# Two heads stacked in 64 columns instead of block-diagonal in 128, in the chunk chain of a decoder layer

## The chip, the core and the metric

The kernel runs on one core of a Trainium2 chip. The core has a matrix engine (PE, with its weight loads shown apart as PEld), three engines for elementwise work (DVE, ACT and POOL), and queues that start transfers between device memory and on-chip memory (SBUF). Matrix products land in PSUM, which PE writes and DVE and ACT read. Every engine works off its own instructions in a fixed order. A wait of one instruction therefore holds up all that stand behind it on that engine. The metric is the device time of one execution in microseconds (us).

## The reference

One decoder layer over 512 positions with 2048 features: a mixing sub-layer and a feed-forward sub-layer, each with a conditioned norm ahead and a gated residual add behind. Half of the mixing features run through a gated linear recurrence (RG-LRU), the other half through 16 heads of 64 features with a matrix state. This second recurrence is what the change touches:

```python
def step(state, inp):
    r_t, d_t, k_t, v_t, kk_t, a_t = inp
    sa = jnp.einsum('bhvk,bhk->bhv', state, -kk_t)
    state = (state * d_t[:, :, None, :]
             + sa[..., None] * (kk_t * a_t)[:, :, None, :]
             + v_t[..., None] * k_t[:, :, None, :])
    y_t = jnp.einsum('bhvk,bhk->bhv', state, r_t)
    return state, y_t
```

## The kernel before

The large products (input projection, output projection, feed-forward) are written as three matmuls each on a rounded and a remainder part of both operands (`mm3`, lines 124 to 126). Their weights are streamed in. ACT rounds a weight tile (L105) and DVE takes the remainder (L106).

The matrix-state recurrence runs over 8 pairs of heads. One head of a pair has partitions 0 to 63, the other 64 to 127. The 512 positions are cut into 8 chunks of 64, four to a half. For each half of a pair `rwkv_half` builds the operands. `bd_a`, `bd_bt`, `bd_v` and `bd_xt` are block-diagonal tiles of 128 columns a chunk, one 64 by 64 block for each head and zeros elsewhere. `inverse` finds the inverse of a triangular 32 by 32 block by 31 steps of two short DVE instructions each (L764 and L766), in which each step needs the one before. The transposed input of the steps is the tile `rw_at` (L757), their result is transposed to `rw_xn` (L768), and PE needs that for L783.

`rwkv_chain` then goes over the chunks. Each has four links: `w` (L694, L696, copied out by ACT at L698), `u` (L701, copied out at L703), the new state (L708, L709, combined on DVE at L720 with the old state scaled by ACT at L719), and three matmuls into the output `yps` (L710, L712, L713). All eight matmuls take 128 by 128 weights. `w`, `u` and the state are 128 columns wide, and the output matmuls move 64 columns.

The order is written by `weave`. It goes round five generators (the chain, the two halves, the pair's set-up, and the modulation columns) and a filler, which is the large products. Each generator yields how long PE is thought to work and how long its result is thought to take. Until that time is over, filler is put in, three matmuls at a time. The recording layer then moves instructions of each engine by its own estimates, so the final order is not the written one. PSUM tile `ch` has two buffers.

## Time and profile before

| | |
|---|---|
| median of 3 runs | 2511.21 us (2509.33 to 2516.2) |
| profiled execution | 2503.34 us, span 2501.5 us |
| PE busy, whole span | 2403.7 us (96%) |
| DVE busy, whole span | 1380.6 us (55%) |
| stage of the recurrence | 250 to 915 us |
| PE, DVE, ACT, POOL busy in that stage | 638.14, 566.14, 326.33, 71.67 of 665 us |

A matmul on plain 32-bit operands appears as two records with two weight loads, so "x2" in the timeline is one matmul of the program. The end of a matmul is modelled, and starts of successive matmuls tell more about their price than durations. "PE busy" therefore covers small gaps between starts.

### The profile page before, as it was taken

To read this page: it belongs to the slowest core of one execution; us is meant where nothing else is said; L and a number is where in the kernel's file an instruction comes from. 1 tells how busy PE (TensorE), PEld (TensorE's weight loads), DVE (VectorE), ACT (ScalarE), POOL (GpSimd) and SP (SyncE) were. 2 spreads that over 40 slices of the span, in tenths; PEclk is the share of its full clock that TensorE was granted. 3 is DMA by queue.
4 is the path that set the end of the run, shared out by engine and by line. 5 is a ranking of instruction groups with operands and counts; after the bars stand their busy time and mean duration, and the time that the engine had idled before them with its cause. 6 is when DMAs were issued, how large, how long until landed. Compare 5 with 4: busy or idle time off the path is not lost.

```text
span 2501.5 us, 30983 instructions
## 1 busy us (share of the span) xinstructions
PE 2403.7 (96%) x11560; PEld 1951.2 (78%) x11560; DVE 1380.6 (55%) x3111; ACT 843.9 (34%) x1340; POOL 82.5 (3%) x131
## 2 busy tenths in 40 slices
PE   6999999999999999999999999999999999999997
PEld 3677777877777877788788888888888888888885
DVE  7879898999979838855423322233322233222244
ACT  4357364465365333422222222222222222222221
POOL 0000111111101100000000000000000000000000
PEclk9999999999999999999999999999999999999998
DMA  8864444444442438366423332323333233332233
GB/s 313 307 220 129 146 126 152 130 150 150 132 129 88 136 118 286 105 213 203 149 86 96 107 98 97 99 85 95 109 98 97 91 93 107 98 99 96 86 95 114
DMA packets 138938, 333.22 MB, mean 133 GB/s; under 512 B 15458, under 2 KB 28898, under 8 KB 134690
## 3 DMA queue, kind: packets, MB, share of 16 engines
q1 hardware_dynamic: 138788, 331.25, 41.0%
q8 instruction: 90, 1.47, 0.2%
q14 instruction: 60, 0.49, 0.1%
HBM read 322.92 MB, written 7.87 MB: 132 GB/s over the span
## 4 chain that ended last, share of the span: by engine, by line
PE 69%; DVE 10%; DMA 8%; issue 1%; ACT 1%; SPq 0%; POOL 0%; DVEq 0%; ACTq 0%
PE ps_mm L124 9%; PE ps_mm L126 9%; PE ps_mm L125 9%; DMA adaq<-in_w_ada 6%; PE ps_gr L126 6%; PE ps_gr L124 6%; PE ps_gr L125 6%; PE ps_st L124 6%; PE ps_st L126 6%; PE ps_st L125 6%; DVE adaq L199 2%; DVE wlo L106 2%; DVE rw_xp L764 1%; DVE rw_x L766 1%; DMA wraw<-in_w_out 1%
## 5 line engine op out<-in xcount | busy, mean ns | idle before, releaser
L106 DVE TENSOR_TENSOR wlo<-wraw,whi 128x1024 fp32r<-128x1024 f32 (+2 forms) x552 | 497.1, 902 | 727.6 <-ACT whi L105 718.9
L105 ACT CAST whi<-wraw 128x1024 fp32r<-128x1024 f32 (+2 forms) x552 | 436.7, 793 | 1286.3 <-PE ps_mm L125 398.0
L124 PE MATMUL ps_mm<-hhi,whi 128*128 128x512 f32 x1020 | 415.7, 409 | 9.5 <-ACT hhi L251 6.9
L126 PE MATMUL ps_mm<-hhi,wlo 128*128 128x512 f32 x1020 | 406.6, 399 | 0.1
L125 PE MATMUL ps_mm<-hlo,whi 128*128 128x512 f32 x1020 | 405.6, 398 | 0.9 <-DVE hlo L252 0.7
L124 PEld LDWEIGHTS ps_mm<-hhi,whi 128*128 128x128 f32 x1020 | 193.3, 190 | 51.3 <-ACT hhi L251 9.2
L125 PEld LDWEIGHTS ps_mm<-hlo,whi 128*128 128x128 f32 x1020 | 193.6, 190 | 43.1 <-DVE hlo L252 5.1
L126 PEld LDWEIGHTS ps_mm<-hhi,wlo 128*128 128x128 f32 x1020 | 193.4, 190 | 40.6 <-issue 1.1
L199 DVE SCALAR_TENSOR_TENSOR adaq<-adaq,cbq 128x512 f32<-128x512 f32 x256 | 173.7, 688 | 87.2 <-DMA adaq<-in_w_ada 80.9
L124 PE MATMUL ps_st<-hhi,whi 128*128 128x512 f32 x496 | 194.2, 392 | 1.6 <-ACT hhi L251 1.6
L126 PE MATMUL ps_st<-hhi,wlo 128*128 128x512 f32 x496 | 193.7, 391 | 1.8 <-DVE wlo L106 1.8
L126 PE MATMUL ps_gr<-hhi,wlo 128*128 128x512 f32 x496 | 193.6, 390 | 0.9 <-DVE wlo L106 0.9
L125 PE MATMUL ps_gr<-hlo,whi 128*128 128x512 f32 x496 | 193.5, 390 | 0.0
L125 PE MATMUL ps_st<-hlo,whi 128*128 128x512 f32 x496 | 193.5, 390 | 0.0
L124 PE MATMUL ps_gr<-hhi,whi 128*128 128x512 f32 x496 | 192.8, 391 | 0.0
L124 PEld LDWEIGHTS ps_st<-hhi,whi 128*128 128x128 f32 x496 | 93.6, 189 | 21.7 <-ACT hhi L251 2.2
L126 PEld LDWEIGHTS ps_st<-hhi,wlo 128*128 128x128 f32 x496 | 93.4, 188 | 21.9 <-DVE wlo L106 2.7
L126 PEld LDWEIGHTS ps_gr<-hhi,wlo 128*128 128x128 f32 x496 | 93.4, 188 | 20.8 <-DVE wlo L106 1.3
L124 PEld LDWEIGHTS ps_gr<-hhi,whi 128*128 128x128 f32 x496 | 93.8, 189 | 19.6
L125 PEld LDWEIGHTS ps_st<-hlo,whi 128*128 128x128 f32 x496 | 93.5, 188 | 19.9 <-DVE hlo L252 0.3
L125 PEld LDWEIGHTS ps_gr<-hlo,whi 128*128 128x128 f32 x496 | 93.4, 188 | 19.6
L766 DVE TENSOR_TENSOR rw_x<-rw_x,rw_xp 128x27 f32<-128x27 f32 (+23 forms) x496 | 95.0, 197 | 5.7
(312 smaller groups left out, 3804.8 us busy)
## 6 DMA issues: line engine op xcount, KB each, us to landing
wraw<-in_w_gu SPq DMA_DIRECT2D x176, 512.0 KB, 3.6
adaq<-in_w_ada SPq DMA_DIRECT2D x256, 256.0 KB, 3.3
wraw<-in_w_in SPq DMA_DIRECT2D x160, 256.0 KB, 3.0
ada<-in_w_ada SPq DMA_DIRECT2D x32, 1024.0 KB, 7.2
wraw<-in_w_down SPq DMA_DIRECT2D x64, 512.0 KB, 3.4
wraw<-in_w_out SPq DMA_DIRECT2D x64, 256.0 KB, 3.2
wraw<-in_w_down SPq DMA_DIRECT2D x64, 192.0 KB, 2.3
x<-in_x SPq DMA_DIRECT2D x32, 256.0 KB, 5.4
```

Of the source, the lines that this page charges most:

```text
L105: nc.scalar.copy(out=hi, in_=src)
L106: nc.vector.tensor_tensor(out=lo, in0=src, in1=hi.bitcast(F32), op=ALU.subtract)
L124: mm(ps, lhsT=w[0], rhs=x[0], start=start, stop=False)
L125: mm(ps, lhsT=w[0], rhs=x[1], start=False, stop=False)
L126: self.pe = mm(ps, lhsT=w[1], rhs=x[0], start=False, stop=stop).ins
L199: nc.vector.scalar_tensor_tensor(out=t, in0=t, scalar=1.0, in1=cb, op0=ALU.mult, op1=ALU.mult, accum_out=part[:, m, h:h + 1])
L764: tt(out=pr[:, :n, :j], in0=at[:, s + 1:, s:s + 1].to_broadcast([P, n, j]), in1=x[:, s:s + 1, :j].to_broadcast([P, n, j]), op=ALU.mult)
L766: tt(out=x[:, s + 1:, :j], in0=x[:, s + 1:, :j], in1=pr[:, :n, :j], op=ALU.add)
```

## The change

`w`, `u` and the state become 64 columns wide, with one head in partitions 0 to 63 and the other below it. Their weights (`bd_bt`, `bd_a`, `bd_xt`, `kn`, `bn`) stay 128 by 128, which keeps the heads apart. The three output matmuls still need block-diagonal weights from `v`, `u` and the state. These are now copied into tiles of their own:

- `v` is copied out of PSUM once, whole, into `rw_vs` by ACT. POOL copies its two blocks to `bd_v` (before, ACT did it in two instructions, L628).
- `u` is copied out by ACT three times: once whole, and once for each block of `bd_u`.
- The new state is copied into `bd_s` by two POOL instructions.

The state update is written ahead of the output matmuls, and the durations that the chain yields to `weave` are smaller. The tile `rw_at` has one buffer for both halves where it had one for each. `rw_xn`, which lived in the same buffer, has one of its own for each half.

```diff
+        for nm in ("u", "s"):
+            self.bd[nm] = [rw.tile([P, P], F32, name=f"bd_{nm}{z}") for z in range(2)]
...
+        vs = rw.tile([P, 4, C], F32, tag="vs", name="rw_vs", bufs=2)
+        nc.scalar.copy(out=vs, in_=pv[:, :, :C])
         for g in range(2):
             rows, cols = slice(g * C, g * C + C), slice(g * C, g * C + C)
-            nc.scalar.copy(out=bvv[rows, :, cols], in_=pv[rows, :, :C])
+            nc.gpsimd.tensor_scalar(out=bvv[rows, :, cols], in0=vs[rows], scalar1=1.0,
+                                    scalar2=None, op0=ALU.mult)
...
-            ps = self.ps("ch")[:, :P]
-            mm(ps, lhsT=bt, rhs=bvv, start=True, stop=c == 0)
+            ubd, sbd = self.bd["u"][c % 2], self.bd["s"][c % 2]
+            ps = self.ps("ch")[:, :C]
+            mm(ps, lhsT=bt, rhs=vs[:, cc], start=True, stop=c == 0)
             if c:
-                mm(ps, lhsT=ba, rhs=sbd, start=False, stop=True)
-            w = small("w", 1)
+                mm(ps, lhsT=ba, rhs=sst, start=False, stop=True)
+            w = small("w", 1)[:, :C]
             nc.scalar.copy(out=w, in_=ps)
-            yield 0.43, HOP, None
-            ps = self.ps("ch")[:, :P]
+            yield 0.3, HOP, None
+            ps = self.ps("ch")[:, :C]
             mm(ps, lhsT=xt, rhs=w, start=True, stop=True)
-            u = small("u")
+            u = rw.tile([P, C], F32, tag="u", name="rw_u", bufs=2)
             nc.scalar.copy(out=u, in_=ps)
-            yield 0.21, HOP, None
+            for g in range(2):
+                rows = slice(g * C, g * C + C)
+                nc.scalar.copy(out=ubd[rows, rows], in_=ps[rows])
+            yield 0.15, HOP, None
+            if c < NCH - 1:
+                ps = self.ps("ch")[:, :C]
+                mm(ps, lhsT=kn[:, cc], rhs=vs[:, cc], start=True, stop=False)
+                mm(ps, lhsT=bn[:, cc], rhs=u, start=False, stop=True)
...
+                    stt(out=snew, in0=ps, scalar=pc, in1=sp, op0=ALU.mult, op1=ALU.add)
...
+                for g in range(2):
+                    rows = slice(g * C, g * C + C)
+                    nc.gpsimd.tensor_scalar(out=self.bd["s"][1 - c % 2][rows, rows], in0=sst[rows], scalar1=1.0,
+                                            scalar2=None, op0=ALU.mult)
+                yield 0.3, LSN / 2, None
             yo = yps[:, c * C:(c + 1) * C]
...
             mm(yo, lhsT=bvv, rhs=rkt[:, cc], start=True, stop=False)
             if c:
                 mm(yo, lhsT=sbd, rhs=ar[:, cc, C:], start=False, stop=False)
-            mm(yo, lhsT=u, rhs=gb[:, cc, C:], start=False, stop=True)
+            mm(yo, lhsT=ubd, rhs=gb[:, cc, C:], start=False, stop=True)
...
-            yield 1.07, LSN, None
+            yield 0.5, LSN / 2 - 0.5, None
...
-        at = rw.tile([P, 32, 32], F32, tag=f"at{hf}", name="rw_at")
+        at = rw.tile([P, 32, 32], F32, tag="at", name="rw_at")
...
-        xn = rw.tile([P, 32, 4], F32, tag=f"at{hf}", name="rw_xn")
+        xn = rw.tile([P, 32, 4], F32, tag=f"xn{hf}", name="rw_xn")
```

The instructions move on three engines. The first place is PE in the first half of the first pair's chain, from the `u` matmul of one chunk to that of the next. Before (L701 `u`; L708, L709 new state; L694, L696 `w` of the next chunk; L710, L712, L713 output; L124 to L126 large products):

```order
L701 MATMUL ps_ch<-rw_w,bd_xt_1406 128x128
L708 MATMUL ps_ch<-bd_v_1402,rw_kn 128x128
L124 MATMUL ps_mm<-hhi,whi 128x512
L709 MATMUL ps_ch<-rw_u,rw_bn 128x128
L713 MATMUL ps_y<-rw_gb,rw_u 128x64
L694 MATMUL ps_ch<-bd_v_1402,bd_bt_1398 128x128
L710 MATMUL ps_y<-rw_rkt,bd_v_1402 128x64
L125 MATMUL ps_mm<-hlo,whi 128x512
L126 MATMUL ps_mm<-hhi,wlo 128x512
L124 MATMUL ps_mm<-hhi,whi 128x512
L696 MATMUL ps_ch<-rw_s,bd_a_1394 128x128
L712 MATMUL ps_y<-rw_ar,rw_s 128x64
```

And now, from the same link (L709 `u`; L718, L719 new state; L702, L704 `w`; L735, L737, L738 output):

```order
L709 MATMUL ps_ch<-rw_w,bd_xt_1406 128x64
L718 MATMUL ps_ch<-rw_vs,rw_kn 128x64
L126 MATMUL ps_mm<-hhi,wlo 128x512
L719 MATMUL ps_ch<-rw_u,rw_bn 128x64
L124 MATMUL ps_mm<-hhi,whi 128x512
L738 MATMUL ps_y<-rw_gb,bd_u_1411 128x64
L702 MATMUL ps_ch<-rw_vs,bd_bt_1398 128x64
L735 MATMUL ps_y<-rw_rkt,bd_v_1402 128x64
L125 MATMUL ps_mm<-hlo,whi 128x512
L704 MATMUL ps_ch<-rw_s,bd_a_1394 128x64
L737 MATMUL ps_y<-rw_ar,bd_s_1414 128x64
```

Between the state's second matmul and the matmul that reads the new state there stood three large ones, and now stand two. The output matmul that reads the state, right behind, now reads POOL's copy.

The second place is DVE, where the inverse of a second half begins (`STREAM_TRANSPOSE` into `rw_at`) and that of the first half of the same pair ends (into `rw_xn`). Before, third pair:

```order
L757 STREAM_TRANSPOSE rw_at<-rw_dg 128x1024
L764 TENSOR_TENSOR rw_xp<-rw_at,rw_x 128x8
L745 TENSOR_TENSOR rw_t_3895<-rw_t_3895,ps_ch 128x512
L766 TENSOR_TENSOR rw_x<-rw_x,rw_xp 128x8
L764 TENSOR_TENSOR rw_xp<-rw_at,rw_x 128x31
L684 TENSOR_TENSOR rw_lws<-rw_w,rw_lws 32x128
L764 TENSOR_TENSOR rw_xp<-rw_at,rw_x 128x4
L766 TENSOR_TENSOR rw_x<-rw_x,rw_xp 128x31
```

Now, the same pair:

```order
L779 TENSOR_TENSOR rw_xp<-rw_at,rw_x 128x4
L205 TENSOR_TENSOR mod<-mod,vecs 128x16
L199 SCALAR_TENSOR_TENSOR adaq,adaparts<-adaq,cbq 128x512
L781 TENSOR_TENSOR rw_x<-rw_x,rw_xp 128x4
L772 STREAM_TRANSPOSE rw_at<-rw_dg 128x1024
L783 STREAM_TRANSPOSE rw_xn<-rw_x 128x128
L779 TENSOR_TENSOR rw_xp<-rw_at,rw_x 128x31
```

The steps of the two halves stood between one another (a step of 8 next to one of 31). Now the second half's tile is filled only when the first half's last step has been read, and no two neighbouring steps belong to different halves anywhere in the program.

The third place is POOL, where a pair's chain is copied aside (`bd_s`), with the copies for later halves (`bd_v`, `bd_a`, `bd_xt`) between. Before, POOL had `bd_a` (L616), `bd_xt` (L775) and a few memsets alone. Now, fourth pair:

```order
L790 TENSOR_SCALAR bd_xt_1407<-rw_xs 32x4x32 x4
L731 TENSOR_SCALAR bd_s_1415<-rw_s 64x64 x2
L731 TENSOR_SCALAR bd_s_1414<-rw_s 64x64 x2
L634 TENSOR_SCALAR bd_v_1403<-rw_vs 64x4x64 x2
L731 TENSOR_SCALAR bd_s_1415<-rw_s 64x64 x2
L620 TENSOR_SCALAR bd_a_1395<-rw_ar 64x4x64 x2
```

The pair's last two state copies stand behind the two `bd_v` copies of the next pair.

## The prediction

> **What bounds the kernel now.** I read the page first. PE is busy 96% of the span, so only what PE does or waits for counts. Then comes the recurrence's stage, 250 to 915 us, in the view by stretches of time (columns: stretch, its length, then busy us of PE, PEld, DVE, ACT and POOL, each with its count, then PE's clock, DMA share and GB/s), and then the waits (who waited for whom: total us, times, longest).

> ```profile
> PE 2403.7 (96%) x11560; PEld 1951.2 (78%) x11560; DVE 1380.6 (55%) x3111; ACT 843.9 (34%) x1340; POOL 82.5 (3%) x131
> 250.00:915.00 665.00, 638.14 (x3864) 516.58 (x3863) 566.14 (x1878) 326.33 (x651) 71.67 (x104) 0.97 0.41 130
> PE ps_gr L783 <- DVE rw_xn L768: 19.6, 10, 4.6
> PEld ps_ch L709 <- ACT rw_u L703: 5.8, 26, 0.4
> ```

> In this stage PE is idle 27 us of 665, and 19.6 of these are ten waits for DVE to end an inverse. There are 16 inverses. DVE is busy 85%, so it is a second limit close behind PE: PE runs ahead of it until L783. The chain of chunks shows in the last row, 26 waits of 0.2 us of a weight load for the copy of `u`. ACT and POOL have room.

> **Fewer columns on PE: 0.** In a pair, L694 and L701 run for all 8 chunks, and L696, L708 and L709 for 7, which makes 37, or 296 over 8 pairs. All are now half as wide. The timeline has 128-column and 64-column matmuls in one chunk (columns: start, duration from the first record's start, line).

> ```profile
> 868.09 0.38 PE L708 MATMUL ps_ch<-bd_v,rw_kn 128*128 128x128 f32 x2
> 868.31 0.39 PE L709 MATMUL ps_ch<-rw_u,rw_bn 128*128 128x128 f32 x2
> 868.54 0.33 PE L710 MATMUL ps_y<-rw_rkt,bd_v 128*128 128x64 f32 x2
> 868.71 0.39 PE L712 MATMUL ps_y<-rw_ar,rw_s 128*128 128x64 f32 x2
> 868.93 0.39 PE L713 MATMUL ps_y<-rw_gb,rw_u 128*128 128x64 f32 x2
> 869.13 0.48 PE L124 MATMUL ps_mm<-yhi,whi 128*128 128x512 f32 x1
> 869.44 0.40 PE L125 MATMUL ps_mm<-ylo,whi 128*128 128x512 f32 x1
> 869.68 0.40 PE L126 MATMUL ps_mm<-yhi,wlo 128*128 128x512 f32 x1
> ...
> 868.21 0.30 PEld L709 LDWEIGHTS ps_ch<-rw_u,rw_bn 128*128 128x128 f32 x2
> 868.43 0.30 PEld L710 LDWEIGHTS ps_y<-rw_rkt,bd_v 128*128 128x128 f32 x2
> 868.65 0.30 PEld L712 LDWEIGHTS ps_y<-rw_ar,rw_s 128*128 128x128 f32 x2
> ```

> The two wide ones take 868.54-868.09 = 0.45, or 0.225 each. The three narrow ones and the large one behind them take 869.44-868.54 = 0.90. A large one alone takes 0.24 (869.68-869.44), which leaves 0.66, or 0.22 each. The widths cost the same, and the weight loads say why: each matmul needs two, and they follow at 0.22 a pair whatever is moved. The change leaves all weights 128 by 128 and all matmuls in place, so PE's work stays as it is. I take 0. The other bound is what moving half as much would save if nothing else limited it. A 512-column plain matmul (L568) gives that price.

> ```profile
> L568 PE MATMUL ps_st<-rw_t,cons 128*128 128x512 f32 x16 | 9.3, 665 | 4.2 <-ACT rw_t L566 4.2
> 354.41 0.91 PE ps_st L568 x2
> ```

> Its two records take 0.91 us on the chain at 354.41, so 64 columns are 0.91/8 = 0.11, and 296 of them 33 us. Range of this term: -33 to 0.

> [...]

> **The `u` link: -2.6.** Order and cover stay: one state matmul and one large one stand between `u` and the matmul that needs it. The link, from L701 to L709, took 0.74 us in this chunk:

> ```profile
> 476.54 0.38 PE L701 MATMUL ps_ch<-rw_w,bd_xt 128*128 128x128 f32 x2
> 477.28 0.49 PE L709 MATMUL ps_ch<-rw_u,rw_bn 128*128 128x128 f32 x2
> ```

> It gets shorter. The narrow matmul ends earlier by 0.38-0.33 = 0.05 (rows above), and the copy is smaller.

> ```profile
> L703 ACT COPY rw_u<-ps_ch 128x128 f32<-128x128 f32 x64 | 16.9, 265 | 36.3 <-PE ps_ch L701 36.0
> L657 ACT COPY rw_kn<-ps_st 128x512 f32<-128x512 f32 x16 | 9.4, 586 | 6.0 <-PE ps_st L655 5.9
> L720 DVE SCALAR_TENSOR_TENSOR rw_s<-ps_ch,rw_pcs,rw_w 128x128 f32<-128x128 f32 x48 | 16.6, 346 | 2.9 <-PE ps_ch L709 2.7
> L969 DVE SCALAR_TENSOR_TENSOR x<-ps_gr,mod,x 128x512 f32<-128x512 f32 x22 | 16.5, 751 | 28.3 <-PE ps_gr L126 28.3
> ```

> ACT's slope is (586-265)/384 = 0.84 ns a column, so 64 columns are 0.05. Together 0.10, so the link becomes 0.64, and 26 waits give -2.6; bounds -5.8 (all of the wait) and 0. The `w` link loses a large matmul of cover but is as much shorter, so nothing is put down for it. The two extra copies of `u` stand behind the one that PE waits for. Their reader (L738) stands 0.22 x 3 + 0.23 x 2 = 1.1 us behind `u`, and the copies need about 0.64 + 2 x 0.2, so 0; if ACT is held up by a weight cast, up to +6. ACT itself gets 128 more short copies, some 30 us in a stage where it idles over 330.

> **The state link: +2.** The same chunk's link goes on from L709 at 477.28:

> ```profile
> 478.12 0.34 DVE L720 SCALAR_TENSOR_TENSOR rw_s<-ps_ch,rw_pcs,rw_w 128x128 f32<-128x128 f32 x1
> 478.52 0.49 PE L696 MATMUL ps_ch<-rw_s,bd_a 128*128 128x128 f32 x2
> ```

> It takes 1.24 us. DVE's slope is (751-346)/384 = 1.05 ns a column, so its part shrinks by 0.07 and the matmul's by 0.05, which makes 1.12. In the new order four narrow and two large matmuls stand between, 4 x 0.22 + 2 x 0.23 = 1.34, where one more large one stood. It is just covered, with less left when DVE is late. I take 0.05 at 40 places, +2; bounds 0 and +8.

> **The state's copy on POOL: +8.** This wait is new. L737 needs `bd_s`, and behind it on PE stands the whole chain and all large products. The trace has POOL copies of other sizes.

> ```profile
> L775 POOL TENSOR_SCALAR bd_xt<-rw_xs 32x128 f32<-32x128 f32 x64 | 40.4, 631 | 286.9 <-DVE rw_xs L771 162.8 <-DVE rw_xp L764 102.9 <-DVE rw_x L766 17.8
> L616 POOL TENSOR_SCALAR bd_a<-rw_ar 64x256 f32<-64x256 f32 x32 | 34.6, 1082 | 251.0 <-DVE rw_xp L764 121.8 <-DVE rw_ar L609 104.0 <-PE ps_mm L124 12.7
> ```

> The slope is (1082-631)/128 = 3.5 ns an element, so a 64-element copy takes 0.41 and the two 0.82. From the state's second matmul: 1.06 to the state's end (1.18 before, less 0.12), 0.82, and two handovers of 0.06 as from DVE to PE above, 2.0 us. Counted in the new order, 33 of 56 such places have 1.8 us of PE work or less between, 0.2 to 0.4 short. 33 x 0.3 is 10, less what the `w` link behind it would have waited anyway; I take +8. Bounds: 0 (DVE prompt, POOL at its shortest) and 33 x 0.5 = +16.

> **DVE: +17 of work, +10 on PE.** Halving the state saves 56 x 0.07 = 4. Two things add. First, a step of the inverse waits for the one before it, but another half's step does not.

> ```profile
> 481.17 0.21 DVE L764 TENSOR_TENSOR rw_xp<-rw_at,rw_x 128x26 f32<-128x26 f32 x1
> 481.41 0.20 DVE L766 TENSOR_TENSOR rw_x<-rw_x,rw_xp 128x26 f32<-128x26 f32 x1
> ...
> 506.77 0.16 DVE L766 TENSOR_TENSOR rw_x<-rw_x,rw_xp 128x12 f32<-128x12 f32 x1
> 506.85 0.20 DVE L764 TENSOR_TENSOR rw_xp<-rw_at,rw_x 128x31 f32<-128x31 f32 x1
> 506.97 0.68 DVE L199 SCALAR_TENSOR_TENSOR adaq<-adaq,cbq 128x512 f32<-128x512 f32 x1
> ```

> Steps of one half follow at 0.24, and a step is followed by foreign work after 0.08 to 0.12. Neighbours of one half go from 310 to 411 in the order, neighbours of two halves from 173 to 0, and steps with other work behind from 509 to 581. That is 101 x 0.24 - 173 x 0.11 + 72 x 0.11 = +13. Second, a short step that meets a POOL copy is held.

> ```profile
> 575.20 2.44 POOL L616 TENSOR_SCALAR bd_a<-rw_ar 64x256 f32<-64x256 f32 x2 [18.88 <-DVE rw_ar L609]
> 575.47 0.39 DVE L766 TENSOR_TENSOR rw_x<-rw_x,rw_xp 128x36 f32<-128x36 f32 x1
> 575.90 0.20 DVE L764 TENSOR_TENSOR rw_xp<-rw_at,rw_x 128x34 f32<-128x34 f32 x1
> ```

> It lasted 0.39 instead of 0.20. There are 112 + 32 = 144 more POOL copies. The steps are about a third of DVE's time and DVE is busy 85%, so 144 x 0.19 x 0.33 x 0.85 = +8. Sum: -4 + 13 + 8 = +17. Of the 16 inverses 10 found PE waiting, so 10/16 of it reaches PE, +10; bounds 0 and +17. While PE waits in the chain (2 + 8 - 2.6 = 7), DVE catches up, which by the same share takes back 4.6.

> **Sum.** 0 - 2.6 + 2 + 8 + 10 - 4.6 = +12.8 on the profiled 2503.3 (its span of 2501.5 and 1.8 around it), 2516. The three runs' median, 2511.2, is 7.9 above that execution, so on the runs I expect 2524.

> **Rivals.** (1) The narrow matmuls are cheaper after all: 33 us less on PE, the rest as above, 2524 - 33 = 2491. For it: shorter durations of L710. Against: the starts. 6%.

> (2) Faster because the first half's inverse ends sooner. Before, the second half's transpose and steps are mixed into its end:

> ```profile
> 503.43 2.08 DVE L757 STREAM_TRANSPOSE rw_at<-rw_dg 128x1024 f32<-128x1024 f32 x1
> 509.07 0.39 DVE L768 STREAM_TRANSPOSE rw_xn<-rw_x 128x128 f32<-128x128 f32 x1
> 509.52 0.67 PE L783 MATMUL ps_gr<-rw_xn,rw_gb 32*32 32x32 f32 x16 [2.21 <-DVE rw_xn L768]
> ```

> If the inverses end before PE comes, the 19.6 us of waits go, and with the chain's +7 that is -12: 2499. It decides once half of those waits vanish. Against it: the new order still has that transpose of 2 us just ahead of the first half's end, and more DVE work. 11%.

> (3) No difference to be seen: DVE's 99 idle us in the stage take the added work and the chain's terms cancel, +2: 2513. 25%.

> (4) POOL's queue holds the chain up. In two pairs the last state's copies stand behind `bd_v` copies that wait for PE and ACT, 2 x 1.08 us and that wait. With all short places at 0.5 (+16), DVE's full +17 and 2 x 3 for those, less 2.6, it is +36: 2547. 13%.

> **Chances.** The forecast has 45%, with +5 to +22 as its own range. What a measurement can tell from no change is about 0.3%, 7.5 us. Faster holds (1) and (2), 17%. Within holds (3) and a fifth of the forecast, 33%. Slower is the rest, 50%. The range leaves out (1), a part of (2) and the end of (4): 2500 to 2543.

> **What would show it.** Right: starts of L708's and L709's successors still 0.22 apart; L737 waiting for POOL `bd_s`, some 0.3 us each; DVE's steps longer in all; L783 still waiting some 20 us or more; PE's idle in the stage up by 10 to 20 us. Wrong: PE's starts closer than 0.2 us in the chain (1), no wait at L783 (2), or no wait for POOL at all (3). The forecast fails if the recorded order hides the POOL copy better than 1.8 us of cover tells.

## The result, and the profile after

The changed kernel takes 2572.43 us (median of 4 runs, 2571.13 to 2576.72). The kernel before took 2510.27 us beside it (2505.62 to 2516.2). The ratio is 1.0248, 95% interval 1.0232 to 1.0264: 62 us slower. The prediction had 2524, with a range up to 2543. The direction was right and the size was not: five times the +13 of the sum.

The profiled execution took 2573.44 us. First the page's line on busy time, then the recurrence's stage by stretches of time, then PE's waits between 250 and 985 us, each of the changed kernel. Its line numbers moved: the matmul that needs the inverse, L783, is now L798, and the transpose into `rw_xn`, L768, is now L783.

```profile
PE 2433.4 (95%) x11560; PEld 1972.0 (77%) x11560; DVE 1393.7 (54%) x3111; ACT 859.6 (33%) x1455; POOL 166.6 (6%) x279
```

```profile
250.00:915.00 665.00, 598.62 (x3461) 480.60 (x3462) 542.62 (x1770) 322.02 (x704) 140.96 (x222) 0.94 0.39 123
```

```profile
PE ps_gr L798 <- DVE rw_xn L783: 25.9, 14, 6.3
PE ps_y L737 <- POOL bd_s L731: 20.8, 22, 3.0
PE ps_ch L709 <- POOL bd_xt L790: 6.2, 7, 1.6
PE ps_mm L124 <- ACT lru_g L887: 5.0, 1, 5.0
```

PE has the same 11560 records as before. In the same 665 us it gets through 3461 of them, where before it was 3864. Two things hold it up. It is idle longer: span less busy time is 2571.6 - 2433.4 = 138.2 us over the whole run, against 2501.5 - 2403.7 = 97.8 before, so 40 us more. And the same records take 30 us more of busy time, because the granted clock is lower. The view of the core has span and mean clock, before and after:

```profile
core 0: 2501.5 us, clock 0.987
```

```profile
core 0: 2571.6 us, clock 0.977
```

By these, 0.013 x 2501.5 = 33 us of clock were lost before and 0.023 x 2571.6 = 59 after, 27 more. Idle time (40) and clock (27) make 67 of the 70 us between the two spans. The prediction's sum had PE's waits. It had no term for the clock.

How the two hang together is seen at the longest wait for `bd_s`. POOL's timeline has its queue, DVE's the state that POOL copies, PE's the wait.

```profile
485.95 2.42 POOL L620 TENSOR_SCALAR bd_a<-rw_ar 64x256 f32<-64x256 f32 x2 [1.03 <-DVE rw_ar L613]
488.44 1.75 POOL L634 TENSOR_SCALAR bd_v<-rw_vs 64x256 f32<-64x256 f32 x2
490.27 0.81 POOL L731 TENSOR_SCALAR bd_s<-rw_s 64x64 f32<-64x64 f32 x2
```

```profile
486.67 0.28 DVE L725 SCALAR_TENSOR_TENSOR rw_s<-ps_ch,rw_pcs,rw_w 128x64 f32<-128x64 f32 x1
```

```profile
491.13 0.43 PE L737 MATMUL ps_y<-rw_ar,bd_s 128*128 128x64 f32 x2 [3.00 <-POOL bd_s L731]
...
493.15 0.63 PE L124 MATMUL ps_mm<-hhi,whi 128*128 128x512 f32 x1
493.57 0.63 PE L125 MATMUL ps_mm<-hlo,whi 128*128 128x512 f32 x1
...
496.47 0.39 PE L124 MATMUL ps_mm<-hhi,whi 128*128 128x512 f32 x1
496.69 0.39 PE L125 MATMUL ps_mm<-hlo,whi 128*128 128x512 f32 x1
```

The state was there at 486.95. POOL was busy with the next half's `bd_a` and `bd_v` and came to it at 490.27, so PE stood for 3.00 us. After that the large matmuls start 0.42 apart instead of 0.22, until some 3.4 us later they are back. Three stretches of the same time show what they ran on (the third figure from the end is PE's clock):

```profile
489.01:492.42 3.41, 1.29 (x9) 1.16 (x10) 1.64 (x7) 0.00 (x0) 1.85 (x4) 1.00 0.48 142
492.42:495.84 3.42, 3.42 (x10) 2.65 (x10) 2.12 (x7) 1.10 (x2) 0.00 (x0) 0.50 0.10 23
495.84:499.25 3.41, 3.41 (x17) 2.81 (x16) 1.82 (x7) 1.21 (x2) 0.00 (x0) 1.00 0.57 210
```

PE was busy for 1.29 of 3.41 us, and the next 3.41 us ran at half the clock, 10 records where 17 fit. The stop cost its 3.00 us and then about 1.7 more, half of that stretch. The kernel before shows the same behind a wait for an inverse:

```profile
505.99:509.39 3.40, 1.32 (x6) 0.75 (x4) 3.40 (x19) 1.21 (x2) 0.00 (x0) 1.00 0.60 169
509.39:516.21 6.82, 6.69 (x45) 5.04 (x46) 4.82 (x19) 3.57 (x7) 2.19 (x4) 0.50 0.62 200
```

So it could have been read before the prediction was made. The view by stretches was read there with one row for the whole stage, and its 0.97 averages over stretches of 0.50.

### The profile page after: what moved, and what is told of

Its sections match the earlier page's. It is cut to its first block, busy times and chain, and to the rows that moved or that the text cites. A ratio compares the mean times of both kernels' runs of the same rounds, so it can differ in the third digit from the quotient of the medians.

```text
span 2571.6 us, 31252 instructions
## 1 busy us (share of the span) xinstructions
PE 2433.4 (95%) x11560; PEld 1972.0 (77%) x11560; DVE 1393.7 (54%) x3111; ACT 859.6 (33%) x1455; POOL 166.6 (6%) x279
## 4 chain that ended last, share of the span: by engine, by line
PE 66%; DVE 13%; DMA 8%; issue 2%; POOL 2%; ACT 2%; DVEq 0%; SPq 0%; ACTq 0%; POOLq 0%
PE ps_mm L124 8%; PE ps_mm L125 8%; PE ps_mm L126 8%; DMA adaq<-in_w_ada 6%; PE ps_gr L126 6%; PE ps_gr L124 6%; PE ps_gr L125 6%; PE ps_st L126 6%; PE ps_st L125 6%; PE ps_st L124 6%; DVE wlo L106 2%; DVE adaq L199 2%; DVE rw_xp L779 1%; DVE rw_x L781 1%; POOL bd_s L731 1%
## 5 line engine op out<-in xcount | busy, mean ns | idle before, releaser
L124 PE MATMUL ps_mm<-hhi,whi 128*128 128x512 f32 x1020 | 413.6, 407 | 13.3 <-ACT hhi L251 6.9
L125 PE MATMUL ps_mm<-hlo,whi 128*128 128x512 f32 x1020 | 413.9, 406 | 1.0 <-DVE hlo L252 0.9
L126 PE MATMUL ps_mm<-hhi,wlo 128*128 128x512 f32 x1020 | 412.4, 404 | 0.7 <-DVE wlo L106 0.6
L124 PEld LDWEIGHTS ps_mm<-hhi,whi 128*128 128x128 f32 x1020 | 195.9, 192 | 56.0 <-ACT hhi L251 9.2
L125 PEld LDWEIGHTS ps_mm<-hlo,whi 128*128 128x128 f32 x1020 | 196.1, 192 | 44.8 <-DVE hlo L252 5.1
L126 PEld LDWEIGHTS ps_mm<-hhi,wlo 128*128 128x128 f32 x1020 | 195.8, 192 | 42.0 <-issue 1.9
L199 DVE SCALAR_TENSOR_TENSOR adaq<-adaq,cbq 128x512 f32<-128x512 f32 x256 | 174.1, 689 | 83.1 <-DMA adaq<-in_w_ada 76.2
L124 PE MATMUL ps_st<-hhi,whi 128*128 128x512 f32 x496 | 194.0, 391 | 1.6 <-ACT hhi L251 1.6
L126 PE MATMUL ps_gr<-hhi,wlo 128*128 128x512 f32 x496 | 193.5, 390 | 1.4 <-DVE wlo L106 1.3
L126 PE MATMUL ps_st<-hhi,wlo 128*128 128x512 f32 x496 | 193.7, 390 | 1.2 <-DVE wlo L106 1.2
L125 PE MATMUL ps_st<-hlo,whi 128*128 128x512 f32 x496 | 193.4, 390 | 0.0
L125 PE MATMUL ps_gr<-hlo,whi 128*128 128x512 f32 x496 | 193.3, 390 | 0.0
L124 PE MATMUL ps_gr<-hhi,whi 128*128 128x512 f32 x496 | 192.7, 391 | 0.0
L124 PEld LDWEIGHTS ps_st<-hhi,whi 128*128 128x128 f32 x496 | 93.5, 188 | 21.5 <-ACT hhi L251 2.2
L126 PEld LDWEIGHTS ps_gr<-hhi,wlo 128*128 128x128 f32 x496 | 93.3, 188 | 21.7 <-DVE wlo L106 2.2
L126 PEld LDWEIGHTS ps_st<-hhi,wlo 128*128 128x128 f32 x496 | 93.4, 188 | 21.3 <-DVE wlo L106 2.0
L124 PEld LDWEIGHTS ps_gr<-hhi,whi 128*128 128x128 f32 x496 | 93.7, 189 | 19.4
L125 PEld LDWEIGHTS ps_st<-hlo,whi 128*128 128x128 f32 x496 | 93.3, 188 | 19.9 <-DVE hlo L252 0.3
L125 PEld LDWEIGHTS ps_gr<-hlo,whi 128*128 128x128 f32 x496 | 93.4, 188 | 19.6
L779 DVE TENSOR_TENSOR rw_xp<-rw_at,rw_x 128x24 f32<-128x24 f32 (+23 forms) x496 | 99.7, 201 | 7.5
```

What stands on the lines that cost most here:

```text
L124: mm(ps, lhsT=w[0], rhs=x[0], start=start, stop=False)
L125: mm(ps, lhsT=w[0], rhs=x[1], start=False, stop=False)
L126: self.pe = mm(ps, lhsT=w[1], rhs=x[0], start=False, stop=stop).ins
L199: nc.vector.scalar_tensor_tensor(out=t, in0=t, scalar=1.0, in1=cb, op0=ALU.mult, op1=ALU.mult, accum_out=part[:, m, h:h + 1])
L779: tt(out=pr[:, :n, :j], in0=at[:, s + 1:, s:s + 1].to_broadcast([P, n, j]), in1=x[:, s:s + 1, :j].to_broadcast([P, n, j]), op=ALU.mult)
```

## The experiments

The times of the runs are given as a ratio to the kernel before on the same chip, with its 95% interval, and in us of that kernel's 2510.

### One part left out or done alone

The first run leaves the state's copies out of the changed kernel:

```diff
-                for g in range(2):
-                    rows = slice(g * C, g * C + C)
-                    nc.gpsimd.tensor_scalar(out=self.bd["s"][1 - c % 2][rows, rows], in0=sst[rows], scalar1=1.0,
-                                            scalar2=None, op0=ALU.mult)
```

> This kernel is the changed one without the two POOL copies of the state per chunk: `bd_s` stays at zero, so the output matmul of the state multiplies zeros (that part of y is left out); every matmul, every other copy and the order of writing stay. (A) The wait for POOL is the main cause: the profile of the changed kernel has 21 us of PE waits for `bd_s` in the recurrence's stage, and the gaps cost clock besides; all of it goes, with what POOL does to DVE: 2573 becomes 2530 to 2545. (B) DVE's serialised inverse is the main cause: only the 112 POOL copies that hold DVE's short steps go, some 5 to 10 us: 2563 to 2568. (C) The new order with a matmul chain that has less behind each handover is the main cause: the wait for POOL is replaced by the next wait behind it in the chain, 2560 to 2570.

Measured: 1.0198 (1.0171 to 1.0224). Against the changed kernel that is 0.5%, or 13 us less, where (A) asked for 27 or more. It comes to 2560 us, the lower edge of (C). PE's waits in the recurrence's stage say where the rest stays:

```profile
PE ps_gr L794 <- DVE rw_xn L779: 29.6, 15, 4.8
PE ps_ch L709 <- POOL bd_xt L786: 8.4, 7, 1.6
```

The 20.8 us of waits for `bd_s` are gone, but PE comes earlier to the inverse and waits there 3.7 us longer than in the changed kernel, and 2.2 longer for `bd_xt`. So the state's copy is one cause, but less than a quarter of the loss.

Then two parts of the change alone in the kernel before. The first is the new order, with the state's matmuls and update ahead of the output matmuls:

```diff
-            yield 0.43, HOP, None
+            yield 0.3, HOP, None
...
-            yield 0.21, HOP, None
+            yield 0.15, HOP, None
...
+                sbd = snew
+                yield 0.3, LSN / 2, None
             yo = yps[:, c * C:(c + 1) * C]
...
-            yield 1.07, LSN, None
+            yield 0.5, LSN / 2 - 0.5, None
```

> This kernel is the one before (128 columns, no copies aside) with the state move written ahead of the output matmuls and the three planner times of the changed kernel. (A) POOL's copy is the cause: no POOL copy here, so 2510 to 2516. (B) The single buffer of the inverse is the cause: two buffers here, 2510 to 2516. (C) The order is the cause: 2535 to 2560.

Measured: 1.0045 (1.0032 to 1.0059), +11 us, between what (A) and (B) have and what (C) asked for. The waits for the inverse did not grow by it (16.7 us in 6, before 19.6 in 10); waits for other results of DVE, ACT and POOL did.

The second is the single `rw_at`:

```diff
-        at = rw.tile([P, 32, 32], F32, tag=f"at{hf}", name="rw_at")
+        at = rw.tile([P, 32, 32], F32, tag="at", name="rw_at")
-        xn = rw.tile([P, 32, 4], F32, tag=f"at{hf}", name="rw_xn")
+        xn = rw.tile([P, 32, 4], F32, tag=f"xn{hf}", name="rw_xn")
```

> This kernel is the one before with one buffer for the inverse's `rw_at` and `rw_xn` in a buffer of its own per half, and nothing else. (A) POOL's copy is the cause: 2510 to 2516. (B) The serialised inverse is the cause: the prediction put it at 13 us of DVE time, 8 of them on PE, and if it is the main term it must be more: 2530 to 2550. (C) The order is the cause: 2510 to 2516.

Measured: 1.0082 (1.0057 to 1.0108), +21 us, at the lower edge of (B). It is the largest of these three parts. Its inverse waits grew, as did the one for `bd_xt` (PE's waits in the same stage, and then the row on `bd_xt` of the kernel before):

```profile
PE ps_gr L783 <- DVE rw_xn L768: 23.6, 13, 4.3
PE ps_ch L701 <- POOL bd_xt L775: 4.8, 4, 1.6
```

```profile
PE ps_ch L701 <- POOL bd_xt L775: 0.2, 1, 0.2
```

The edits of both together:

> This kernel is the one before with two parts of the change: the new order and planner times, and the single `rw_at` with `rw_xn` apart; 128 columns, no copies aside. The parts alone were +11 and +21 us. (A) They add up: 2535 to 2542. (B) They share a cause (the inverse comes late in either): no more than the larger alone, 2525 to 2532. (C) They make each other worse, because a chain that stops more often meets an inverse that ends later: 2548 to 2560.

Measured: 1.0099 (1.0080 to 1.0119), +25 us, or 2535, where (A) begins and 3 us above (B). (C) is out. Whether the two add up is not settled: alone they make 11 + 21 = 32, and the intervals reach that far. A shared cause, a late inverse, is not shown either, since the order alone did not raise the waits for it.

### Which engine copies

The chain wide again and block-diagonal, with all copies aside kept (`rw_vs` with one buffer, for room):

```diff
-            ps = self.ps("ch")[:, :C]
-            mm(ps, lhsT=bt, rhs=vs[:, cc], start=True, stop=c == 0)
+            ps = self.ps("ch")[:, :P]
+            mm(ps, lhsT=bt, rhs=bvv, start=True, stop=c == 0)
```

> This kernel is the changed one with its chain 128 columns wide and block-diagonal again: w, u and the state are 128 by 128 and bd_v is the moved operand, while the copies aside, the order and the planner's times stay. (A) and (C), and the prediction's price of 0 for the columns: nothing is gained or lost on PE by 128 columns, the links are as long as before, 0.05 to 0.2 us more at 40 places: 2573 to 2583. (D) Narrow matmuls did gain on PE what the prediction's rival (1) gives, 33 us, and hid a still larger loss: 2600 to 2610. (E) The narrow matmuls cost time, by the granted clock or otherwise: 2545 to 2560.

Measured: 1.0220 (1.0190 to 1.0251), 7 us less than the changed kernel, with intervals that overlap. (D) is out: the narrow columns hid no gain of 33 us. Between (A) and (E) it does not decide, and the runs on columns below take that up.

Next, `bd_v` copied by ACT again and the state by POOL (the first edit alone), and then both by ACT:

```diff
-            nc.gpsimd.tensor_scalar(out=bvv[rows, :, cols], in0=vs[rows], scalar1=1.0,
-                                    scalar2=None, op0=ALU.mult)
+            nc.scalar.copy(out=bvv[rows, :, cols], in_=pv[rows, :, :C])
...
-                    nc.gpsimd.tensor_scalar(out=self.bd["s"][1 - c % 2][rows, rows], in0=sst[rows], scalar1=1.0,
-                                            scalar2=None, op0=ALU.mult)
+                    nc.scalar.copy(out=self.bd["s"][1 - c % 2][rows, rows], in_=sst[rows])
```

> This kernel is the changed one with `bd_v` copied by ACT out of PSUM as before the change; the state's copies stay on POOL. By the runs so far the change's +62 us hold about 11 for the order, 21 for the single `rw_at` and 13 for the state's copies, which leaves some 17 for the rest. (A) The rest is POOL's: 32 `bd_v` copies of 0.94 us stand in POOL's queue ahead of `bd_s` and `bd_xt`, which PE waits for (6.2 us at L709 for `bd_xt`): 2553 to 2562, and the PE waits for `bd_xt` and `bd_s` fall to under 18 us together. (B) The rest lies in the parts acting on each other (a stage whose clock is lower as it stops more often): 2568 to 2576, with the same waits.

> This kernel is the changed one with both the `bd_v` and the `bd_s` copies on ACT, so that POOL does what it did before the change. (A) POOL was the wrong engine for these copies: what the state's removal gave (13 us) and what `bd_v` costs come back together, 2535 to 2550; what stays over the time before is the order and the single buffer, 32 us. (B) The copies' place is indifferent, since what PE doesn't wait for at L737 it waits for at the next inverse: 2555 to 2565, with the waits for `rw_xn` at 28 us or more.

The first gave 1.0280 (1.0226 to 1.0333), with single executions from 2556 to 2587. (A) of it fails, and its median lies above (B) too: `bd_v` off POOL alone brings no time. The waits for `bd_s` and `bd_xt` came to 12.0 and 8.9 us, above the 18 of (A). But PE did wait less. In the profile it is idle for 2583.3 - 2453.6 = 129.7 us, 8.5 less than in the changed kernel. What was gained there went to the clock: at 0.971 it lost 75 us, 16 more. Of one and the same program, the execution of 2556 us had a clock of 0.984 and the two longest had 0.971, so here the clock made a difference of 30 us from one execution to the next. What sets it apart was not found.

The second gave 1.0122 (1.0101 to 1.0143), +31 us, or 32 less than the changed kernel: (A). PE's idle time fell by 31 us against the changed kernel and the clock's loss by 8.5. With the order and the single buffer (+25) nearly all of what stays is accounted for. By difference, the narrow chain with its copies costs some 6 us where ACT makes them (not clear of the noise) and some 37 where POOL makes those of `v` and the state. No run moved the state's copies to ACT alone, so how the 32 us divide between the two moves stays open.

Does POOL's work as such cost the time, or PE's wait for it? In this run POOL copies the state but PE reads a constant:

```diff
-                mm(yo, lhsT=sbd, rhs=ar[:, cc, C:], start=False, stop=False)
+                mm(yo, lhsT=self.con("ident"), rhs=ar[:, cc, C:], start=False, stop=False)
```

> This kernel is the changed one, POOL's copies of the state included, but the output matmul of the state reads a constant matrix in place of `bd_s` (that part of y is left out of the computation), so that PE never waits for the copies. Without the copies it was 2557.7, with them read 2572. (A) PE's wait for `bd_s` is what they cost: 2553 to 2562. (B) POOL's work as such costs it, by holding DVE's short operations and POOL's own queue: 2568 to 2576.

Measured: 1.0195 (1.0179 to 1.0211), the same as without the copies (1.0198). (A): what the state's copies cost is PE's wait for them. That they may also hold DVE's short steps costs nothing that can be seen.

### The narrow chain by itself

Against the kernel before, the first of the next two runs has the chain of the change in 64 columns and constants for y:

```diff
             ba, bt, bvv, xt = (self.bd[n][hf][:, cc] for n in ("a", "bt", "v", "xt"))
+            ubd = sbd = bvv = self.con("ident")
```

> This kernel has the narrow chain alone: w, u and the state in 64 columns, with the planner's times of before, two `rw_at` buffers as before and `bd_v` copied by ACT. Nothing is copied aside: the output matmuls read a constant matrix in place of `bd_v`, `bd_s` and `bd_u` (so y is left out of the computation, with the same matmuls in count and shape); the state's second matmul still stands ahead of the output matmuls. (A) Columns are worth nothing on PE and the links a little, as the prediction had it: 2500 to 2510. (B) Columns are worth up to 33 us and other parts of the change hid it: 2473 to 2490. (C) The narrow matmuls themselves cost time: 2520 to 2535.

The second makes the operands of y, with ACT:

```diff
-            ubd = sbd = bvv = self.con("ident")
+            ubd, sbd, bvv = (self.bd[n][c % 2] for n in "usv")
...
+            for g in range(2):
+                rows = slice(g * C, g * C + C)
+                nc.scalar.copy(out=ubd[rows, rows], in_=ps[rows])
+                nc.scalar.copy(out=bvv[rows, rows], in_=vs[rows, cc])
...
+                for g in range(2):
+                    rows = slice(g * C, g * C + C)
+                    nc.scalar.copy(out=self.bd["s"][1 - c % 2][rows, rows], in_=sst[rows])
```

> This kernel keeps the narrow chain with valid operands for y, and undoes all else: two `rw_at` buffers, the planner's times of before, and all copies aside on ACT. `bd_v` is copied per chunk by ACT into two 128 by 128 buffers in place of two for four chunks each, which frees the room for the second `rw_at`. ACT does 64 x 6 short copies of about 0.2 us where before it did 32 of 0.4. (A) The narrow chain gains some 8 us as the run with constants in y had it, and ACT's copies cost no more than they did behind the new order (2537 against 2532): 2498 to 2510. (B) ACT's 64 us more work holds up the copies of w and u that PE waits for: 2515 to 2530.

The narrow chain with constants in y gave 0.9969 (0.9951 to 0.9987), -8 us: (A). With these operands made by ACT it gave 1.0028 (1.0011 to 1.0046), +7 us, or 2517, the lower end of (B). So making y's block-diagonal operands costs more than the narrow chain gains, even with nothing else changed. That the gain of the first run comes from shorter links is not shown: its y waits for no copy, and in its profile PE's idle time fell by 3 us only (95.0 against 97.8), while a higher clock (0.992 against 0.987) gave 13. No run of the narrow chain with the operands of y made beats the kernel before.

The waits for the inverse suggested another way to a faster kernel, one time of the planner:

```diff
-INVLAT = 30.2
+INVLAT = 38.0
```

> The kernel before with one planner time changed: the matmuls behind an inverse are placed 38 us after its start in place of 30.2. (A) The waits for `rw_xn` (19.6 us in ten) and the half clock behind them come from a place that is too early: both go, 2475 to 2495. (B) What the inverse's matmuls wait less for, the chain behind them waits more, or the large products run out earlier: 2505 to 2525.

Measured: 1.0068 (1.0044 to 1.0092), +17 us, or 2527, just above (B). The wait at L783 fell from 19.6 to 5.2 us, and others took its place, in the large products and the chain itself (PE's waits in that stage):

```profile
PE ps_st L568 <- ACT rw_t L566: 11.2, 4, 5.2
PE ps_mm L124 <- ACT yhi L105: 10.8, 2, 9.9
PE ps_ch L701 <- ACT rw_w L698: 6.7, 6, 4.0
PE ps_gr L783 <- DVE rw_xn L768: 5.2, 5, 1.8
```

### What a stop of PE costs

Links of a small matmul, an ACT copy and a matmul that reads it were put in 44 places of the last stage of the kernel before. This is the form with one link; the other has four:

```diff
+                x = self.ones[:, :C]
+                for _ in range(1):
+                    p = self.ps("ch")[:, :C]
+                    nc.tensor.matmul(p, lhsT=self.con("ident"), rhs=x, start=True, stop=True)
+                    x = fp.tile([P, C], F32, tag="dz", name="dz", bufs=2)
+                    nc.scalar.copy(out=x, in_=p)
+                p = self.ps("ch")[:, :C]
+                nc.tensor.matmul(p, lhsT=self.con("ident"), rhs=x, start=True, stop=True)
```

> This kernel is the one before with 44 stops of PE put into the last stage, one after each pair of gate and up products, where PE is otherwise solid: a 64-column matmul, an ACT copy of its result, and a second matmul that reads the copy. Nothing reads the second result. One link of this kind took 0.6 to 0.8 us in the traces so far, plus 0.2 for the two matmuls. (A) A stop costs its own length: 44 x 0.8 to 1.0 is +35 to +44, and the granted clock after 1400 us stays at 1.00. (B) Every stop costs clock too, which the traces so far speak against: of some 300 stretches of 3.4 us with 0.25 to 1.0 us of PE idle, 15 were followed by half the clock: +110 or more.

> The same 44 places with four links in a row, which makes stops of some 2.5 to 3 us, as long as the waits for `rw_xn` and the longest for `bd_s`. (A) A stop costs its own length, as the prediction priced its waits: +110 to +140. (B) A stop of this length also halves the granted clock behind it for 3.4 us or more, as the traces of all runs so far show where PE was idle over 1.75 us of a stretch of 3.4 us (68 of 70 such stretches): 44 x 1.7 to 3.4 us more, +185 to +290, and rows of 0.50 clock after the stops.

Measured: 1.0085 (1.0068 to 1.0102) and 1.0231 (1.0216 to 1.0247). Both fell short of every expectation, since the recording layer had filled the links with large matmuls of the next product and PE did not stop. What they measure is the price of narrow matmuls: 88 of them for 20.4 us and 220 for 56.4, that is 0.23 and 0.26 us each. Moving 64 columns is not cheaper than the 0.22 that the starts showed.

So the order was held: the products of the next step come behind the last small matmul.

```diff
+                with self.tc.issue_after(stop) if f else ExitStack():
                     self.gemm(pg, i["w_gu"][2 * m], h)
                     self.gemm(pu, i["w_gu"][2 * m + 1], h)
```

> As the run with short stops, but the order of PE is held: the gate and up products of the next step come behind the second small matmul, so that nothing fills the link, and PE stops 44 times for one link of about 0.75 us. (A) A stop costs its own length and the two small matmuls cost 0.22 each: 44 x 1.0 to 1.2 is +44 to +53, with the granted clock in the last stage at 1.00. (B) It costs clock too: +110 or more.

> The same with four links in a row, 3.0 us of stop and one more small matmul. (A) A stop costs its own length, as the prediction priced all its waits: 44 x 3.0 to 3.5 is +132 to +154, clock 1.00. (B) The granted clock halves for at least one stretch of 3.4 us behind each, which costs 1.7 us or more besides: +205 to +300, and rows with a clock of 0.50 right behind a stop.

Measured: 1.0302 (1.0282 to 1.0321), +75 us, and 1.0896 (1.0872 to 1.0920), +224 us. PE's timelines of the short and of the long form:

```profile
1521.16 0.33 PE L961 MATMUL ps_ch<-ones,cons 128*128 128x64 f32 x2
1522.34 0.43 PE L965 MATMUL ps_ch<-dz,cons 128*128 128x64 f32 x2 [0.85 <-ACT dz L963]
1522.59 0.48 PE L124 MATMUL ps_gr<-hhi,whi 128*128 128x512 f32 x1
```

```profile
1511.76 0.33 PE L961 MATMUL ps_ch<-ones,cons 128*128 128x64 f32 x2
1512.94 0.43 PE L961 MATMUL ps_ch<-dz,cons 128*128 128x64 f32 x2 [0.85 <-ACT dz L963]
1513.68 0.43 PE L961 MATMUL ps_ch<-dz,cons 128*128 128x64 f32 x2 [0.30 <-ACT dz L963]
1514.41 0.43 PE L961 MATMUL ps_ch<-dz,cons 128*128 128x64 f32 x2 [0.30 <-ACT dz L963]
1515.15 0.61 PE L965 MATMUL ps_ch<-dz,cons 128*128 128x64 f32 x2 [0.30 <-ACT dz L963]
1515.53 0.77 PE L124 MATMUL ps_st<-hhi,whi 128*128 128x512 f32 x1
1516.10 0.63 PE L125 MATMUL ps_st<-hlo,whi 128*128 128x512 f32 x1
```

A short stop takes 1522.59 - 1521.16 = 1.43 us, not the 1.0 to 1.2 expected, and 44 of them 63. The last stage's waits come to 44.1 us rather than 44 x 0.85 = 37.4, which adds 7. That makes 70 of the 75, and the clock stays at 1.00. The time is above (A), but the mechanism is that of (A), with a longer link. Its waits and the last stage by stretches of time:

```profile
PE ps_ch L965 <- ACT dz L963: 44.1, 44, 3.9
```

```profile
1050.00:2450.00 1400.00, 1353.60 (x5990) 1116.75 (x5989) 446.40 (x555) 317.79 (x416) 0.00 (x0) 1.00 0.32 103
```

A long stop takes 1515.53 - 1511.76 = 3.77 us, and 44 of them 166. The other 58 us are the clock, 0.04 x 1550 = 62 by its mean over the last stage. Three stretches of the long form, the stop above, the one right behind it and the whole last stage:

```profile
1511.90:1515.30 3.40, 1.64 (x10) 1.09 (x9) 2.52 (x3) 2.14 (x6) 0.00 (x0) 0.99 0.08 18
1515.40:1518.80 3.40, 3.40 (x10) 2.72 (x10) 0.00 (x0) 0.00 (x0) 0.00 (x0) 0.52 0.40 136
...
1050.00:2600.00 1550.00, 1468.02 (x6246) 1197.69 (x6245) 445.16 (x554) 345.11 (x547) 0.00 (x0) 0.96 0.29 93
```

This is (B). Half clock followed within two stretches of 40 of the 44 long stops, and of 2 of the 44 short ones. A stop of 1.4 us, with one wait of 0.85, costs its length. A stop of 3.8 us costs its length and 1.3 us more, a third on top. PE waits in only 1.75 us of it (0.85 and three times 0.30) and works on small matmuls in the rest.

### Columns and the clock

Half the clock came behind stretches in which PE was busy for little of the time (1.29 of 3.41 us, 1.32 of 3.40 and 1.64 of 3.40 in the rows above). If it follows from how much PE does, a matmul that moves half as much in the same 0.22 us might cost clock. In this run the chain's matmuls move their columns twice:

```diff
-            mm(ps, lhsT=bt, rhs=vs[:, cc], start=True, stop=c == 0)
+            mm(ps2, lhsT=bt, rhs=vs[:, cc].unsqueeze(1).to_broadcast([P, 2, C]), start=True, stop=c == 0)
```

> The changed kernel, but each of its chain's matmuls moves its 64 columns twice, into the two halves of 128 columns of the result, of which only the first is read. PE gets back the 128 columns and nothing else changes: copies, DVE's and ACT's widths and all waits stay (the order that is worked out from modelled times shifts a little). The changed kernel ran at 2572 when the one before ran at 2510, a ratio of 1.0248. (A) Columns cost PE nothing, as the prediction had it: ratio 1.022 to 1.028. (B) They cost what they take to move, the prediction's rival (1): 33 us more, 1.035 to 1.041. (C) PE's clock follows how much PE moves in a stretch of 3.4 us, so that the narrow chain loses clock: the ratio falls to 1.015 to 1.021, and the profile has fewer stretches of half clock.

Measured: 1.0158 (1.0138 to 1.0179): (C). More work for PE, and 23 us less. But the recording layer, which works from modelled times, had ordered the instructions otherwise. In the next two runs the order of every engine is held by a table, so that columns and order are crossed:

```diff
+    for lane in lanes.values():
+        lane.sort(key=lambda ins: rank[ins.name])
+        for prev, ins in zip(lane, lane[1:]):
+            tc.add_manual_dep(ins, prev.name, info, reason="hold_order")
```

> The changed kernel with 64 moved columns, but with every engine's instructions in the order that the run with columns moved twice had (1.0158, against 1.0248 of the changed kernel). So only the order differs from the changed kernel, and only the moved columns from that run. (A) The order made that run faster: 1.013 to 1.019. (B) The moved columns did, through the granted clock: 1.022 to 1.028, with 40 us or so of clock lost as in the changed kernel. Half of each: 1.019 to 1.022.

> The other way round: columns moved twice, with every engine's instructions in the changed kernel's order. (A) The order made the difference: 1.022 to 1.028, as the changed kernel. (B) The moved columns did: 1.013 to 1.019, and fewer stretches of half clock than the changed kernel has. Half of each: 1.019 to 1.022.

| | the changed kernel's order | the other order |
|---|---|---|
| 64 columns | 1.0248 (1.0232 to 1.0264) | 1.0221 (1.0204 to 1.0238) |
| 64 columns twice | 1.0242 (1.0225 to 1.0259) | 1.0158 (1.0138 to 1.0179) |

The first run gave what its (B) has, the columns, and the second what its (A) has, the order. So by the times neither is the cause alone. In the changed order the columns make no difference, in the other one they make 0.6%; the order makes 0.3% with 64 columns and 0.8% with columns twice. The profiles separate the two better. The changed kernel has 20.8 us of waits for `bd_s`, a span of 2571.6 us and a clock of 0.977 (rows above). The same two rows of 64 columns in the other order:

```profile
PE ps_y L737 <- POOL bd_s L731: 10.2, 17, 1.7
```

```profile
core 0: 2560.6 us, clock 0.975
```

Of columns twice in the changed kernel's order:

```profile
PE ps_y L740 <- POOL bd_s L734: 20.6, 23, 3.0
```

```profile
core 0: 2560.5 us, clock 0.982
```

And of columns twice in the other order:

```profile
PE ps_y L740 <- POOL bd_s L734: 9.3, 16, 1.6
```

```profile
core 0: 2549.5 us, clock 0.982
```

The wait goes with the order: 20.8 and 20.6 against 10.2 and 9.3. The clock goes with the columns: 0.977 and 0.975 against 0.982 and 0.982. The mean clock of all executions agrees: 0.978 and 0.976 with 64 columns (four and five executions), 0.981 and 0.983 with columns twice (four each). In profiled span either seems worth 11 us (2571.6, 2560.6, 2560.5, 2549.5), but the four profiles come from three measurements, beside which the kernel before took 2510, 2508 and 2506 us. So the narrow columns do cost clock in the changed kernel, 0.005 to 0.007 in these profiles. In the narrow chain by itself they did not: its mean clock was 0.989, that of the kernel before beside it 0.987. What the columns are worth in time, 0 to 0.6%, was not settled by the medians.

The table bears on the earlier runs too. Those that leave out or move a part left the order to the recording layer, and at some 2000 to 3700 of PE's 11560 places it put another instruction than in the kernel they are compared with. As an order alone made 0.3 to 0.8% here, the price of a single part above may hold 7 to 21 us of order.

## Why the prediction was right or wrong

**Fewer columns on PE: 0.** Right on PE's time. Starts in a chunk of the changed kernel:

```profile
670.44 0.33 PE L738 MATMUL ps_y<-rw_gb,bd_u 128*128 128x64 f32 x2
670.61 0.39 PE L702 MATMUL ps_ch<-rw_vs,bd_bt 128*128 128x64 f32 x2
670.83 0.39 PE L735 MATMUL ps_y<-rw_rkt,bd_v 128*128 128x64 f32 x2
671.03 0.48 PE L124 MATMUL ps_mm<-hhi,whi 128*128 128x512 f32 x1
671.35 0.40 PE L125 MATMUL ps_mm<-hlo,whi 128*128 128x512 f32 x1
```

Three narrow and one large take 0.91. Less 0.24 for the large one, as in the prediction, that is 0.22 each, and the small matmuls put into the last stage gave 0.23 to 0.26. Rival (1) is dead. What the term left out is that the mean clock of the whole run was 0.004 to 0.007 lower with 64 columns than with the same columns moved twice.

**The `u` and state links: -2.6 and +2.** Small, as forecast. The weight load's wait for the copy of `u` fell from 5.8 us in 26 to 0.5 in 2, more than -2.6 and inside the bound. The wait for the state did not grow: 0.5 us at L704, 1.7 at L696 before.

**The state's copy on POOL: +8, bounds 0 to +16.** The mechanism was right, the size too small. The wait was 20.8 us in 22, not 33 x 0.3. Two copies in a row take 0.81 in the row at 490.27, as estimated, but the mean of all is higher, 0.486 each:

```profile
L731 POOL TENSOR_SCALAR bd_s<-rw_s 64x64 f32<-64x64 f32 x112 | 54.4, 486 | 182.1 <-DVE rw_s L725 127.6 <-DVE rw_x L781 34.7 <-DVE rw_xp L779 8.9
```

The larger error was the queue. Five waits of 1.6 to 3.0 us, 12 us in all, stand where `bd_a` or `bd_v` copies are ahead of the state's on POOL, as in the rows of 486 to 491 us. The prediction had this as rival (4), for two pairs only. With no wait on PE for these copies 13 us come back, inside the bounds of the term; with `bd_v` and the state both copied by ACT instead of POOL it is 32 us, far outside.

**DVE: +10 on PE, bounds 0 to +17.** This is the term of the sum that a single run shows most mis-sized. The single `rw_at` alone costs 21 us, over the upper bound, and the prediction passed 10/16 of its 13 us on to PE. Its mechanism is in that run: the 173 steps that followed one of the other half within 0.17 us are gone, and steps of one half follow at 0.22 to 0.24. How 21 us come of it is shown only in part: PE is idle 16 us longer (113.4 against 97.8) and the clock takes 5. Steps that last longer by POOL's copies matter little. A step is 5 ns longer on the mean (L779 201 ns against 195 at L764, L781 199 against 197 at L766), and the run with unread copies shows no cost.

```profile
L779 DVE TENSOR_TENSOR rw_xp<-rw_at,rw_x 128x24 f32<-128x24 f32 (+23 forms) x496 | 99.7, 201 | 7.5
```

**DVE catches up: -4.6.** Right in kind: taking the 20.8 us of waits for `bd_s` away raised those for the inverse and `bd_xt` by 3.7 + 2.2. That is about a quarter, where the prediction took 10/16.

**Not in the sum: the order, and the clock.** The order was read for the links' cover alone. By itself it costs 11 us, with the single buffer 25. The clock is the step that failed for all terms at once: every wait was priced at its own length. The wait of 3.00 us at 491.13 cost some 1.7 more, the forced stops of 3.77 us cost 1.3 more each, and 27 of the 70 us between the spans are clock. The other failure is PE's added idle time: the sum had 13 us in all, and the profile shows 40. The waits for `bd_s` (20.8), the longer waits for the inverse (+6.3) and those for `bd_xt` (+6.0) make 33 of them.

**The rivals.** (2), the waits for the inverse vanish, did not happen: 25.9 us in 14 at L798 against 19.6 in 10. (3) fell with the time. (4) was nearest, with 2547, and named POOL's queue. That its +36 is close to what the copies on POOL cost (32 to 37 us) is chance: 17 of the 36 are DVE's.

**What stays open.** The state's copies cost 13 us when they alone are taken out, `bd_v` back on ACT alone brought nothing, and both off POOL brought 32. No run separates this, and what sets the clock of one execution apart from the next of the same program was not found. The prices of single parts hold the order that each run got.

## What to carry to other kernels

Before pricing a new wait on a dense matrix engine, look at the clock in stretches of some 3.4 us around the waits that are there already, not at its mean over a stage; if it reads 0.50 behind them, a wait as long as those costs more than its length (here 1.3 to 1.7 us more for stops of 3 to 4 us), while 44 stops with one wait of 0.85 us cost only themselves. A copy that is cheap in busy time can be dear on an engine whose queue also holds long or waiting copies (here two copies of 0.81 us together, behind others of 2.42 and 1.75, held PE for 3.00): count what can be ahead of it, not only its own duration. And take one buffer away from a serial helper chain only after asking which two instances interleaved through it, since here that one buffer cost 21 us by itself.

## What the runs showed of the hardware that was not expected

Half clock does not always end after one step, even where PE has no wait: of some 155 half-clock steps with under 0.25 us idle, 51 were followed by another. Weighed by columns moved (the 512 columns of a large matmul with one record as 0.23 us of full work, a plain one's as 0.91), a step in this stage was followed by half clock always under 1.0 us of such work and never from 2.4 up (14 profiles, the two kernels and the first twelve runs; in those of the two kernels alone 11 steps of 11 and none of 303). That is a count over records and not an experiment. It fits that moving the columns twice raised the mean clock by 0.005 to 0.007 at about the same waits, and that the long forced stops, with 1.75 us of waits among small matmuls, were followed by half clock in 40 of 44 cases. It does not explain why the narrow chain by itself lost no clock (0.989 against 0.987).
